# Placing small fp32 products next to each other on TensorE, with a price for each change of kind in the planner's clock

## The chip, the cores and the metric

The program runs on one core of one Trainium2 chip. The metric is device time of one execution in microseconds (us). The kernel before takes 1213.42 us, the median of 3 runs (1213.35 to 1214.24).

The engines are named as in the profile: PE is TensorE (its matrix products and transposes), PEld its weight loads, DVE VectorE, ACT ScalarE, POOL GpSimd, SP SyncE, whose queue issues the transfers.

## The reference

It is a decoder trunk of two layers on 256 positions of width 1024, in float32. A layer is a half-step SwiGLU feed-forward block, a token mixer with three branches side by side, and a second feed-forward block, with a layer norm behind each:

```python
for i in range(DEPTH):                                   # DEPTH = 2
    x = layer_norm(DN_ALPHA * x + 0.5 * swiglu(x, ...))  # gate, up 1024x2816, down 2816x1024
    h = x @ w_in[i]
    z_gmlp, z_qk, z_v, z_s5, z_gate = split(h)
    y_a = gmlp_mixer(z_gmlp, ...)        # gelu, layer norm, causal 128x128 spatial product per group
    y_b = diff_attention(q, k, v, ...)   # 4 heads, softmax(q1 k1) - lam * softmax(q2 k2), causal, rms norm
    y_c = s5_mixer(z_s5, ...)            # complex diagonal scan over time, then a gated linear unit
    mix = sum_k(sigmoid(z_gate[k]) * (y_k @ w_branch[k])) @ w_out
    x = layer_norm(DN_ALPHA * x + mix)
    x = layer_norm(DN_ALPHA * x + 0.5 * swiglu(x, ...))
```

## The kernel before

All weights pass once through the core, 202 blocks ("pairs") of 128x2048 numbers. One transfer brings a block into `raw`; ACT rounds it to fp32r (`wh`, two casts), DVE subtracts to get the remainder (`wl`, two subtractions), and PE multiplies in fp32r: activation-high by weight-high, activation-low by weight-high, activation-high by weight-low. These are the main products, nearly all with 512 or 256 columns. They are one stream in a fixed order.

Beside them PE has small products in plain fp32, whose results other engines wait for. These are 128x128 transposes (`trx` of a normed x, `trh` of a feed-forward activation, `trw` in the preparation of the scan, `tra` of softmax weights, `tro` of attention output, `trm` of the mix) and the products of the branches: `psg<-wsT,vn` (the spatial product of gMLP; the other `psg` are main products of the gates), `pss` (attention scores), `po` (weights by values), `bu` (input of the scan), `py` (output of the scan), `pk`. Tiles are named so in the trace; one fp32 product other than a transpose shows as two MATMUL rows there.

The mixer works like this. DVE turns `bu` by a table (`t`), scans it (`gr`, `gi`) and turns it back (`Hr`, `Hi`), in four blocks; each block's `py` needs `Hr` and `Hi`. An attention step is `pss` on PE, masked maxima on DVE (`sm<-pss`), exponentials on ACT, reciprocals and the weighted difference on DVE (`sm<-sm`), `tra` on PE, a copy on ACT (`at`), `po` on PE. There are four steps of two heads each. The gMLP product goes through DVE twice (`psg<-psg,bsr`, `uv<-uv,psg`) before its PSUM bank is free. `bu`, `py`, `pss`, `po` and the gMLP product share four PSUM banks (`acc`, line 329); `pss` and `bu` take two at once.

Which instruction comes next is decided when the program is built. Every piece of work is a Python generator (a stream) that hands out operations. `Scheduler.run` (line 282) keeps a clock per engine, estimates when each stream's next operation could start (`ready`, line 202; durations from `Engine.cost`, line 119), and issues the one that can start first, by priority where they tie. Engines then run their instructions in that order, whatever the chip's real times are; a semaphore makes an instruction wait, and all behind it on its engine. On PE an operation that isn't of the main stream is taken only if the estimate has its operands ready for 0.5 us already (`SLACK`, line 300). A transpose is put at 0.107 us, an fp32 product of n columns at 0.0017 n, times 0.46 where it has at most 64 output rows (lines 125 and 128). Most operations are recorded at line 222, where the call is made, so that groups are told apart by tile.

Of the kernel before, what the change touches and what calls it, by code (L numbers as in the profile page):

```python
# [8 lines left out]
F32 = mybir.dt.float32  # L9
# [27 lines left out]
P_NORM, P_EVAC, P_ATT, P_SSM, P_MAIN, P_PREP = 10, 20, 30, 40, 50, 55  # L37
# [2 lines left out]
P_TURN = 35  # L40
GO = 1

SLACK = 0.5
P_FOLD = P_SSM

# [5 lines left out]
class Op:  # L51


    def __init__(self, eng, calls, cost, ins, outs):
        self.eng, self.calls, self.cost, self.ins, self.outs = eng, calls, cost, ins, outs


class Alloc:
# [91 lines left out]
class Scheduler:  # L150
# [9 lines left out]
    def __init__(self):  # L160
        self.clock = {e: 0.0 for e in self.READY}
        self.streams = []
        self.track = {}
        self.slots = {}
        self.where = {}
        self.index = {}
        self.writer = {}
        self.table = None
        self.seq = 0

    def spawn(self, gen, prio):
# [5 lines left out]
    def times(self, ap):  # L177
# [21 lines left out]
        q = slice(p0 // 32, (p0 + pairs[0][1] + 31) // 32)  # L199
        return arr, q, ix  # L200

    def ready(self, op):
        t = 0.0
        for a in op.ins:
            arr, q, ix = self.times(a)
            t = max(t, arr[0, q, ix].max())
        for a in op.outs:
            arr, q, ix = self.times(a)
            if self.writer.get(a.tensor.name) == op.eng:
                t = max(t, arr[1, q, ix].max())  # L210
            else:
                t = max(t, arr[:, q, ix].max())
        return t + (0.1 if op.eng == "PE" else 0.0)

    def issue(self, op, start):
        for _, kw in op.calls:
            held = TABLES.get(kw.get("func"))
            if held is not None and self.table not in held:
                self.table = held[0]
                start += 1.3  # L220
        for fn, kw in op.calls:
            fn(**kw)  # L222
        end = start + op.cost
        self.clock[op.eng] = end
        done = end + self.READY[op.eng]
        for a in op.ins:
            arr, q, ix = self.times(a)
            v = arr[1, q, ix]
            arr[1, q, ix] = v.clip(min=end)
        for a in op.outs:  # L230
            arr, q, ix = self.times(a)
            arr[0, q, ix] = done
            self.writer[a.tensor.name] = op.eng
# [48 lines left out]
    def run(self):  # L282
        while self.streams:
            moved = True
            while moved:
                before = [(id(s), id(s[2])) for s in self.streams]
                self.streams = [s for s in list(self.streams) if self.settle(s)] + \
                    [s for s in self.streams[len(before):]]
                moved = before != [(id(s), id(s[2])) for s in self.streams]
            if not self.streams:  # L290
                break
            best = {}
            for s in self.streams:
                if isinstance(s[2], Op):
                    rd = self.ready(s[2])
                    st = max(self.clock[s[2].eng], rd)
                    pr = s[1]()
                    if s[2].eng == "PE" and pr > P_MAIN:
                        pr = P_MAIN - 1
                    late = SLACK if s[2].eng == "PE" and pr != P_MAIN and self.clock["PE"] > 25 else 0.0  # L300
                    best.setdefault(s[2].eng, []).append((max(st, rd + late), pr, s[3], s, st))
            assert best, ([(s[0].__name__, getattr(s[2], "tag", s[2])) for s in self.streams], self.where)
            pick = None
            for eng, c in best.items():
                first = min(x[0] for x in c)
                urgent = [x for x in c if x[0] <= first + (self.PATIENCE[eng] if x[1] < P_MAIN else 1e-9)]
                x = min(urgent, key=lambda y: (y[1], y[0], y[2]))
                if pick is None or x[0] < pick[0]:
                    pick = x
            self.issue(pick[3][2], pick[4])  # L310
            pick[3][2] = None
# [1373 lines left out]
```

## Time and profile before

| | |
|---|---|
| median of 3 runs | 1213.42 us |
| the profiled execution | 1213.71 us |
| its span, first to last instruction | 1212.0 us |
| PE busy | 1195.5 us, 99% |
| DVE busy | 941.9 us, 78% |
| ACT busy | 697.9 us, 58% |
| mean granted PE clock | 0.997 |

The profiled execution is 1.7 us longer than its span. Each row of a timeline is one instruction, or several of one kind in a row (x8), with its start, the length to the end of the last, and, where the engine sat idle before it, that time and what ended it. PE's products overlap, so their pace is the distance between two starts.

### The profile page before, as it was taken

What the parts mean: (1) busy time and instruction counts of PE and PEld (TensorE: products, weight loads), DVE (VectorE), ACT (ScalarE), POOL (GpSimd) and SP (SyncE); (2) the same over time, 40 slices, a digit from 0 to 9 for tenths busy, and PEclk for the clock granted to TensorE, in tenths of its full rate; (3) what the DMA queues carried; (4) which work ended last, traced back from release to release, by engine and by line L of the source; (5) the groups of instructions that cost most, each with busy time, mean ns of one, the idle gap of its engine ahead of it and who ended that gap; (6) DMA issues with size and microseconds to landing.
All of it is one profiled execution on the core that took longest, in us unless ns stands there. A gap on an engine that the chain in (4) does not pass through costs nothing.

```text
span 1212.0 us, 17132 instructions
## 1 busy us (share of the span) xinstructions
PE 1195.5 (99%) x6504; PEld 1010.8 (83%) x6504; DVE 941.9 (78%) x1696; ACT 697.9 (58%) x1152; POOL 12.9 (1%) x54
## 2 busy tenths in 40 slices
PE   8999999999999999999999999999999999999997
PEld 7888888888788888888888888888877888888886
DVE  5997678889997899876886556697899888765656
ACT  5556566655765565565665555476476657555450
POOL 1000000000000010000000000000000000000000
PEclk9999999999999999999999999999999999999998
DMA  8747765565537466667565555557554574655541
GB/s 313 243 174 243 259 217 209 205 231 188 178 138 278 148 235 208 225 210 256 181 219 198 205 181 202 174 200 256 196 183 155 184 251 163 219 203 205 176 172 35
DMA packets 42851, 245.93 MB, mean 203 GB/s; under 512 B 4880, under 2 KB 5648, under 8 KB 17424
## 3 DMA queue, kind: packets, MB, share of 16 engines
q1 hardware_dynamic: 42480, 244.31, 57.5%
q8 instruction: 51, 0.84, 0.3%
q10 hardware_dynamic: 288, 0.52, 0.2%
q14 instruction: 32, 0.26, 0.1%
HBM read 233.28 MB, written 11.53 MB: 202 GB/s over the span
## 4 chain that ended last, share of the span: by engine, by line
PE 86%; DVE 8%; ACT 3%; DMA 2%; issue 1%; DVEq 0%; ACTq 0%
PE ac L222 23%; PE puc L222 17%; PE pgc L222 16%; PE psg L222 8%; PE psp L222 4%; PE pg L222 3%; PE pu L222 3%; DVE wl L222 3%; PE psc L222 2%; PE ps L222 2%; PE pva L222 2%; PE pvg L222 2%; PE psq L222 1%; DMA raw<-in_wst_dram 1%; ACT wh L222 1%; PE py L222 1%
## 5 line engine op out<-in xcount | busy, mean ns | idle before, releaser
L222 DVE TENSOR_TENSOR wl<-raw,wh 128x1024 fp32r<-128x1024 f32 (+2 forms) x416 | 483.1, 1189 | 151.5 <-ACT wh L222 148.3
L222 ACT CAST wh<-raw 128x1024 fp32r<-128x1024 f32 (+2 forms) x416 | 414.2, 1024 | 259.5 <-DMA raw<-in_wst_dram 102.2
L222 PE MATMUL puc<-xx,wh 128*128 128x512 f32 x576 | 144.7, 393 | 0.0
L222 PE MATMUL pgc<-xx,wh 128*128 128x512 f32 x576 | 143.9, 392 | 0.0
L222 PE MATMUL ac<-wh,hTl 128*128 128x512 f32 (+1 forms) x374 | 141.5, 378 | 0.0
L222 PE MATMUL ac<-wh,hTh 128*128 128x512 f32 (+1 forms) x374 | 141.2, 378 | 0.0
L222 PE MATMUL ac<-wl,hTh 128*128 128x512 f32 (+1 forms) x374 | 140.9, 377 | 0.0
L222 PE MATMUL psg<-wh,xx 128*128 128x512 f32 x384 | 122.3, 400 | 0.0
L222 PEld LDWEIGHTS pgc<-xx,wh 128*128 128x128 f32 x576 | 105.1, 188 | 19.9
L222 PEld LDWEIGHTS puc<-xx,wh 128*128 128x128 f32 x576 | 103.4, 189 | 18.4
L222 PEld LDWEIGHTS puc<-xx,wl 128*128 128x128 f32 x576 | 78.4, 190 | 5.5
L222 PEld LDWEIGHTS pgc<-xx,wl 128*128 128x128 f32 x576 | 78.5, 190 | 5.4
L222 PEld LDWEIGHTS ac<-wl,hTh 128*128 128x128 f32 x374 | 70.3, 188 | 13.2
L222 PE MATMUL pgc<-xx,wl 128*128 128x256 f32 x576 | 81.3, 283 | 0.0
L222 PEld LDWEIGHTS psg<-wh,xx 128*128 128x128 f32 x384 | 69.2, 188 | 14.3 <-issue 0.7
L222 PEld LDWEIGHTS ac<-wh,hTl 128*128 128x128 f32 x374 | 70.5, 188 | 12.3
L222 PE MATMUL puc<-xx,wl 128*128 128x256 f32 x576 | 80.5, 283 | 0.0
L222 PEld LDWEIGHTS ac<-wh,hTh 128*128 128x128 f32 x374 | 70.5, 188 | 11.9
L222 PE MATMUL psg<-wl,xx 128*128 128x512 f32 x192 | 75.0, 391 | 0.0
L222 DVE TENSOR_TENSOR silc<-pgc,cp 128x256 f32<-128x256 f32 x72 | 30.2, 420 | 22.3 <-ACT cp L222 22.2
L222 ACT COPY cp<-pgc 128x256 f32<-128x256 f32 x72 | 26.7, 371 | 33.2 <-PE pgc L222 33.2
L222 DVE TENSOR_TENSOR up<-puc,cp 128x256 f32<-128x256 f32 x72 | 30.3, 421 | 18.2 <-ACT cp L222 17.8
(229 smaller groups left out, 1742.5 us busy)
## 6 DMA issues: line engine op xcount, KB each, us to landing
raw<-in_wst_dram SPq DMA_DIRECT2D x198, 1024.0 KB, 4.9
lngb<-in_lngb_dram SPq DMA_DIRECT2D x12, 512.0 KB, 5.9
raw<-in_wst_dram SPq DMA_DIRECT2D x16, 256.0 KB, 5.7
tbd<-tabw SPq DMA_DIRECT2D x8, 512.0 KB, 6.5
tab<-tbd SPq DMA_DIRECT2D x8, 512.0 KB, 4.5
wbd<-WB SPq DMA_DIRECT2D x4, 512.0 KB, 8.6
cd<-C SPq DMA_DIRECT2D x4, 512.0 KB, 9.3
cf<-cd SPq DMA_DIRECT2D x8, 256.0 KB, 5.9
```

The lines of the kernel that those rows point to most:

```text
L222: fn(**kw)
```

## The change

An operation of PE whose first operand is plain fp32 is marked as a side operation. The planner remembers whether PE's last operation was one. Where the kind changes, 0.14 us are added to the estimated start of the operation. After a side operation the 0.5 us of `SLACK` are not asked of the next one: what the estimate has ready then follows at once.

```diff
+TURN = 0.14
@@ class Op
         self.eng, self.calls, self.cost, self.ins, self.outs = eng, calls, cost, ins, outs
+        self.side = eng == "PE" and ins[0].dtype == F32
@@ class Scheduler
+    def turns(self, op):
+
+        return op.eng == "PE" and op.side != self.side
@@ def issue
+        if op.eng == "PE":
+            start += TURN if self.turns(op) else 0.0
+            self.side = op.side
         end = start + op.cost
@@ def run
-                    late = SLACK if s[2].eng == "PE" and pr != P_MAIN and self.clock["PE"] > 25 else 0.0
+                    late = SLACK if s[2].eng == "PE" and pr != P_MAIN and self.clock["PE"] > 25 and not self.side else 0.0
```

No operation is added or taken away, and the main products keep their order. What moves is the place of the side operations between them, and, since the planner's clocks move, the order on DVE, ACT and SP. Runs of side operations on PE ("islands") go from 92 to 77, changes of kind from 183 to 153.

PE in the first layer's mixer, before, from the gMLP product to the first `tra` (psg_2701 to psg_2876 are the gates' main products):

```order
L222 MATMUL psg<-wsT,vn 128x128 x4
...
L222 MATMUL psg<-wsT,vn 128x128 x4
...
L222 MATMUL pss<-k,q 128x128 x4
...
L222 MATMUL pss<-k,q 128x128 x4
...
L222 MATMUL psg_2876<-wl,xx 128x512
L222 MATMUL tra<-ident,sm 128x128
```

The same stretch after the change:

```order
L230 MATMUL pss<-k,q 128x128 x4
...
L230 MATMUL psg<-wsT,vn 128x128 x4
L230 MATMUL pss<-k,q 128x128 x4
...
L230 MATMUL psg_2708<-wl,xx 128x512
L230 MATMUL psg<-wsT,vn 128x128 x4
L230 MATMUL tra<-ident,sm 128x128 x2
L230 MATMUL psg_2708<-wh,xx 128x512 x2
```

Where rows are left out there are only main products. Between the first `pss` and the first `tra` stood 36 main products, and now stand 21. The first `pss` now comes before both gMLP products, the second directly behind one of them, and both `tra` directly behind the other.

DVE in the same stretch, before, from the first block's `Hi` on:

```order
L222 TENSOR_TENSOR Hi<-u,v 128x4x128
L222 TENSOR_TENSOR wl<-raw,wh 128x1024
L222 TENSOR_TENSOR uv<-psu,cp 128x256
...
L222 TENSOR_TENSOR psg<-psg,bsr 128x512
L222 TENSOR_TENSOR uv<-uv,psg 128x512
...
L222 TENSOR_TENSOR t_2685<-t_2685,t_2686 128x512
L222 ISA sm,ast<-pss,mask 128x128
```

After:

```order
L230 TENSOR_TENSOR Hi<-u,v 128x4x128
L230 TENSOR_TENSOR wl<-raw,wh 128x1024 x2
...
L230 TENSOR_TENSOR t_2621<-t_2621,t_2622 128x512
L230 TENSOR_TENSOR wl<-raw,wh 128x1024
L230 TENSOR_TENSOR uv<-psu,cp 128x256
L230 ISA sm,ast<-pss,mask 128x128
...
L230 TENSOR_TENSOR psg<-psg,bsr 128x512
L230 TENSOR_TENSOR wl<-raw,wh 128x1024
L230 TENSOR_TENSOR uv<-uv,psg 128x512
```

`Hi` has moved ahead of two `wl` that stood before it. The two DVE steps that free the first gMLP product's bank come behind the maxima of the first scores, with a `wl` between them.

PE at the end of that layer's mixer, before (`trx` transposes the first half of the normed x; ac are the main products of the output projection):

```order
L222 MATMUL ac_3878<-wl,mix 128x512
L222 MATMUL trx<-ident,xr_3782 128x128 x8
L222 MATMUL ac_3877<-wh,mix 128x512 x2
L222 MATMUL ac_3877<-wl,mix 128x512
L222 MATMUL ac_3878<-wh,mix 128x512 x2
```

After:

```order
L230 MATMUL ac_3877<-wh,mix 128x512 x2
L230 MATMUL ac_3877<-wl,mix 128x512
L230 MATMUL ac_3878<-wh,mix 128x512 x2
L230 MATMUL ac_3878<-wl,mix 128x512
L230 MATMUL trx<-ident,xr_3782 128x128 x8
```

`trx` comes six main products later. On DVE the last `mix<-trm,mix`, which the next ac products need, has moved from behind the norm of the first half to before it.

## Rows read from the trace of the kernel before

**Rows 1.** The page, part 1: engine, busy us (share of the span), instructions.

```profile
PE 1195.5 (99%) x6504; PEld 1010.8 (83%) x6504; DVE 941.9 (78%) x1696; ACT 697.9 (58%) x1152; POOL 12.9 (1%) x54
```

**Rows 2.** Waits of PE: engine, tile <- what ended it: us, times, longest.

```profile
PE py L222 <- DVE Hi L222: 1.3, 2, 1.0
...
PE tra L222 <- DVE oss L222: 0.4, 2, 0.2
```

**Rows 3.** Timeline of PE, 604 to 619: start, us, instruction, count [idle before].

```profile
604.55 0.40 PE L222 MATMUL ac<-wl,hTh 128*128 128x512 f32 x1
604.78 1.03 PE L222 MATMUL trx<-ident,xr 128*128 128x128 f32 x8
605.57 0.47 PE L222 MATMUL ac<-wh,hTl 128*128 128x512 f32 x1
605.89 0.39 PE L222 MATMUL ac<-wh,hTh 128*128 128x512 f32 x1
...
616.59 0.60 PE L222 MATMUL trx<-ident,xr 128*128 128x128 f32 x4
616.94 0.71 PE L222 MATMUL pu<-wh,xx 128*128 128x512 f32 x2
617.49 0.40 PE L222 MATMUL pu<-wl,xx 128*128 128x512 f32 x1
```

**Rows 4.** Timeline of PE, 280 to 294: scores, then a transpose with `bu`.

```profile
281.02 0.39 PE L222 MATMUL psg<-wl,xx 128*128 128x512 f32 x1
281.34 0.71 PE L222 MATMUL pss<-k,q 64*128 64x128 f32 x8
281.99 0.73 PE L222 MATMUL psg<-wh,xx 128*128 128x512 f32 x2
282.55 0.40 PE L222 MATMUL psg<-wl,xx 128*128 128x512 f32 x1
...
291.99 0.27 PE L222 MATMUL tra<-ident,sm 128*128 128x128 f32 x1
292.19 1.16 PE L222 MATMUL bu<-uu,wbf 64*128 64x128 f32 x16
293.28 0.72 PE L222 MATMUL psg<-wh,xx 128*128 128x512 f32 x2
```

**Rows 5.** Timeline of PE, 413 to 415: transposes of the first mixer's norm.

```profile
413.34 1.36 PE L222 MATMUL trx<-ident,xr 128*128 128x128 f32 x8
414.97 0.73 PE L222 MATMUL ac<-wh,mix 128*128 128x512 f32 x2 [0.26 <-DVE mix L222]
```

**Rows 6.** Timeline of DVE at 414.

```profile
414.23 0.68 DVE L222 TENSOR_TENSOR mix<-trm,mix 128x512 fp32r<-128x512 f32 x1
```

**Rows 7.** Timeline of DVE, 251 to 290: steps of the first mixer.

```profile
251.06 2.07 DVE L222 TENSOR_TENSOR t<-bu,tab 128x256 f32<-128x256 f32 x6
...
263.70 2.36 DVE L222 TENSOR_TENSOR wl<-raw,wh 128x1024 fp32r<-128x1024 f32 x2
...
266.31 0.69 DVE L222 TENSOR_TENSOR Hi<-u,v 128x512 f32<-128x512 f32 x1
...
282.09 0.29 DVE L222 CUSTOM_DVE_ANT_0 sm<-pss,mask 128x128 f32<-128x128 f32 x1
...
283.20 0.69 DVE L222 TENSOR_TENSOR t<-t,t 128x512 f32<-128x512 f32 x1
...
289.32 0.16 DVE L222 RECIPROCAL ast<-ast 128x1 f32<-128x1 f32 x1
...
289.94 0.60 DVE L222 SCALAR_TENSOR_TENSOR sm<-sm,ast 128x128 f32<-128x128 f32 x2
```

**Rows 8.** The page, part 6: transfers, KB each, median us to landing.

```profile
tab<-tbd SPq DMA_DIRECT2D x8, 512.0 KB, 4.5
```

**Rows 9.** Timeline of PE, 862 to 866: output of the second layer's first scan block.

```profile
864.32 0.44 PE L222 MATMUL py<-Hi,cf 128*64 128x129 f32 x4 [1.05 <-DVE Hi L222]
...
865.84 0.50 PE L222 MATMUL psu<-xx,wh 128*128 128x512 f32 x1
```

**Rows 10.** Timeline of ACT at 288: exponentials of an attention step.

```profile
288.43 0.40 ACT L222 ACTIVATE sm<-sm,ast 128x128 f32<-128x128 f32 x1
```

More of the change, by code (lines that the diff above doesn't have):

```diff
@@ L168, in __init__ @@
         self.table = None
+        self.side = False
         self.seq = 0
```

## Prediction

> **What bounds the kernel now.** Read the page's busy times first: PE is busy 1195.5 us of a span of 1212.0, DVE 78%, ACT 58% [rows 1]. Nothing runs beside PE that could become the bound as a whole. Its work is fixed: the same products run in both kernels, so the time is the sum of the main products' pace, the price of the islands of small fp32 products, and PE's waits. Read the waits of PE next: in the mixers 1.3 us before py and 0.4 us before tra, two of each [rows 2]. There is little to win there and, since PE has no idle time to absorb a delay, anything that makes PE wait is paid in full.
>
> Third, the timeline around an island tells what a change of kind costs. A main product of 512 columns starts 0.23 us after the one before (604.55 to 604.78). Eight transposes start at 604.78 and the next main product at 605.57, 0.79 us; that one takes 0.32 instead of 0.23 until the next start, 0.09 more: 0.88 for the island [rows 3]. Four transposes take 0.35 (616.59 to 616.94), and the two main products behind them 0.55 instead of 0.46, 0.09 more: 0.44 [rows 3]. Two islands of four are 0.88 as well. Within the rounding of 0.02 a change of kind in and out is free beside transposes; the planner now reckons 0.28 for it (2 x 0.14).
>
> **What merging saves.** 15 islands fewer at 0 to 0.04 us each: 0 to 0.6, I take 0.3. For islands of products that use half of the array's rows the price is higher: pss begins 0.32 after the main product before it, 0.09 late; it takes 0.65 until the next main start, and the two behind it 0.56, 0.10 late [rows 4]. So 0.19 of the 0.84 are entry and exit. But the change puts these beside full-array products (pss behind psg, tra behind bu, tra behind pss), and there the same entry is due: in the merge that exists already, one tra starts at 291.99, bu only 0.20 later (a transpose's own pace in rows 3 is 0.79/8 = 0.10), and the main product 1.09 after bu [rows 4]. [...]
>
> **What the moved trx saves.** In the tails of both mixers trx comes before its operand: 1.63 us from its start to the next main product, where rows 3 have 0.79 for the same eight [rows 5]. Part of this is the next product's own wait for mix, which DVE has made only at 414.23 to 414.91 [rows 5, 6]. Now trx stands six main products (6 x 0.23 = 1.4 us) later and that mix is made before the norm. Both waits go: 2 x 0.84 = 1.7. What is late next is the feed-forward block that needs these transposes; 42 main products, over 9 us, stood between, 36 remain, 8 us, against two casts and eight activations of ACT, below 6 us by the pace of 0.40 [rows 10].
>
> **What the mixer loses.** Here the order is made anew. Count from the end of the first Hi (0.0), for which py waits, in the order after the change.
>
> DVE: two wl at 1.15 (2.36 for two, overlapping by some 0.06), uv 0.33, wl: 3.8. Then t of the second block, which needs its table: that transfer can only be issued when the first table has been read (0.7 before 0.0), and lands 4.5 later [rows 8]: 3.9. Eight t at 0.345 (2.07 for six) and a uv: 7.0; sum of t 0.6, wl 1.15, uv 0.33: 9.1. The maxima 1.1 (282.09 to 283.20): 10.2; another sum 0.6, wl, psg 0.7, wl, uv 0.65: 14.4. The reciprocals 0.6 (289.32 to 289.94), a remainder ya of 0.65 that waits for a cast of ACT of about as much: 15.8; the two sm 0.6: 16.4 [rows 7].
>
> PE: py ends 1.5 after Hi (864.32 to 865.84) [rows 9]; 28 main products, twelve of 512 and sixteen of 256 columns, 4.6: 6.1. First pss 0.84: 7.0. Nine main products 2.05: 9.0; psg<-wsT, eight rows of 0.10, about 0.9: 9.9. The second pss needs the two banks of the first; of the four one is held by py (its copies come later on ACT) and one by psg, so it waits for the maxima: 10.2, a wait of 0.3, ends 11.0. Twelve main products 2.7: 13.7. The second psg<-wsT needs the bank that uv frees at 14.4: 0.7 wait, ends 15.3. Then tra needs the two sm, ready at 16.4: 1.1 wait. That makes 2.1 at this place.
>
> From there both engines run on from 16.4. DVE: scan 1.15, psg and uv 1.3, scan 1.15, ya 0.6, maxima 0.9, then four exponentials of 0.40 on ACT, reciprocals and sm 0.75: 7.5 to the second step's last tra. PE: nine main products 2.05, po 0.45, nine more 2.05, bu 1.3: 5.9, and one tra. Waits 1.4 in all. By the same walk the third step waits little (39 main products lie ahead of it), the fourth, where tra, bu, po and tra follow each other at once, about 1.9: there po needs an exponential, a copy and a transpose that come 0.4 late, and the last tra stands behind two scans of 1.15 on DVE. Together 5.4 per mixer; the first py waits about 0.4 and 1.2 in the two layers, as DVE reaches Hi some 2.7 earlier and PE too.
>
> That is 2 x 5.4 + 1.6 = 12.4 of waiting. From it goes what waits now: 1.7 as idle time [rows 2], nearer 3 as the length of the islands (in rows 5 idle shows 0.26 of 0.84; an estimate). I take +9.2.
>
> Why the planner does not see it: it reckons 0.28 per island that PE does not spend, and for bu 8 x 0.0017 x 128 = 1.74 where rows 4 have 1.09 to 1.3. So PE comes to a tra earlier than planned, and the 0.5 us of margin that covered this is gone just where operations now follow each other.
>
> **Sum.** +9.2 (mixers) - 1.7 (trx) - 0.3 (islands) = +7.2, and I take 0.7 off, as each link of the walk was counted at its full length: +6.5. On the profiled execution, 1213.7, which is 0.3 above the median, this gives 1220.2, against the median 1219.9. I say 1220. Bounds: if only the first place of each mixer waits, 2 x 2.1 + 1.6 - 3 - 2.0 = +0.8; if the walk is 20% short and nothing is taken off, 12.4 x 1.2 - 3 - 2 = +9.9, and a wait of a main product on top of it up to +11.
>
> **Rivals.** (a) The planner's clocks are right where it counts, and the new order waits no more than the old. For it: PE waits only 1.7 us in both mixers now, so the estimates have been good. Against it: that was with 0.5 us of margin. Then only -1.7 - 0.3 remain: 1211.4, faster by 0.17%. 13%. It wins if the DVE steps between Hi and the first sm take under 14.3 (where PE would arrive unhindered) instead of 16.4. (b) A change of kind costs what the planner says. 30 changes less at 0.14 are 4.2, with trx 5.9, and no new waits: 1207.5. For it only the 0.19 at pss; against it rows 3. 5%. (c) Main products wait too: in the new order heads come before the wl of later gates on DVE, and if a wl comes late, PE's whole stream stands. Each such wl is 1.15; one or two per mixer beyond the forecast make 1223 to 1226. Against it: by the new order the blocks for a gate are finished 8 us or more ahead of it. 8%. (d) The change hardly acts: the islands outside the mixers stay where they were but for trx and trw, and if the two mixers' waits offset each other with what they had, 1213 to 1214. 8%.
>
> **Chances.** My forecast 66%, with a range of its own from 1216 to 1223. What can be told from no change is 0.2%, 2.4 us. Slower by more than that: the forecast but for its lowest twentieth, and (c): 72%. Within: (d), most of (a), the lowest part of the forecast: 19%. Faster: (b) and a part of (a): 9%. The range that holds 8 in 10 goes from 1213 to 1224.
>
> **What would show it.** In the mixers of the new profile, PE waits before tra for DVE sm (about 1 us each, first in each mixer right behind the second psg<-wsT), before psg<-wsT for DVE uv (0.7), and before the last tra behind bu and po; PE's idle time grows by 9 there. The eight trx at the tails take 0.8. Pairs of merged trx take as long as two islands. The forecast is wrong if DVE makes the first sm before PE arrives, or if main products show a shorter pace after fewer islands.

## The result and the profile after

The changed kernel takes 1222.39 us (median of 4, 1221.61 to 1223.38) against 1213.83 for the kernel before in the same comparison: a ratio of 1.0062, with a 95% interval of 1.0050 to 1.0075. It is slower, within the forecast range and 2.4 us above the forecast. The profiled execution took 1221.61, its span is 1219.9.

The page's first part, which answers to [rows 1], does not give the cause: PE is 2.7 us busier with the same 6504 instructions, so a part of its waiting must be counted as busy: the eight `trx` read 1.36 in [rows 5] and 1.03 in the tail below, where they wait for nothing.

```profile
PE 1198.2 (98%) x6504; PEld 1013.3 (83%) x6504; DVE 943.6 (77%) x1696; ACT 699.4 (57%) x1152; POOL 12.0 (1%) x54
```

The waits of PE (tile, what ended the wait: us, times, longest) answer to [rows 2]. PE now waits 4.3 us before `tra` for `sm`, where nothing waited for `sm` before.

```profile
PE tra L230 <- DVE sm L230: 4.3, 6, 1.2
...
PE py L230 <- DVE Hi L230: 1.6, 4, 0.5
...
PE tra L230 <- DVE inv L230: 0.9, 2, 0.5
PE po L230 <- ACT at L230: 0.8, 2, 0.4
```

Both kernels run the same 5666 main products in the same sequence. The start of one product in both traces therefore tells how far the changed kernel is behind at that point:

| main product, place | behind, us | change |
|---|---|---|
| 1200, ahead of the first mixer | 0.79 | +0.8 |
| 1700, first mixer's side work done | 6.31 | +5.5 |
| 1850, first norm's `trx` | 5.41 | -0.9 |
| 1990, first `trh` of the next block | 4.22 | -1.2 |
| 4000, ahead of the second mixer | 4.19 | 0 |
| 4500, second mixer's side work done | 8.87 | +4.7 |
| 4700, second norm's `trx` | 7.93 | -0.9 |
| 5665, last | 7.90 | 0 |

The mixers lose 10.2, the rest gives back 2.3. The timeline of PE at the first merged step of the first mixer (start, length, instruction, count, idle before) shows the loss in place: eight `psg` rows from 279.39, 0.11 apart, the last at 280.24, put the next start by their pace at about 280.35, and `tra` starts 0.7 later; behind `bu` the two `tra` wait one after the other.

```profile
279.39 1.13 PE L230 MATMUL psg<-wsT,vn 128*128 128x128 f32 x8 [0.21 <-DVE inv L230]
281.02 0.57 PE L230 MATMUL tra<-ident,sm 128*128 128x128 f32 x2 [0.51 <-DVE sm L230]
...
286.43 1.16 PE L230 MATMUL bu<-uu,wbf 64*128 64x128 f32 x16
288.03 0.30 PE L230 MATMUL tra<-ident,sm 128*128 128x128 f32 x1 [0.44 <-DVE inv L230]
288.80 0.30 PE L230 MATMUL tra<-ident,sm 128*128 128x128 f32 x1 [0.47 <-DVE sm L230]
...
315.25 0.38 PE L230 MATMUL tra<-ident,sm 128*128 128x128 f32 x2
315.56 1.16 PE L230 MATMUL bu<-uu,wbf 64*128 64x128 f32 x16
317.12 0.71 PE L230 MATMUL po<-uv,at 128*128 128x128 f32 x4 [0.40 <-ACT at L230]
319.02 0.41 PE L230 MATMUL tra<-ident,sm 128*128 128x128 f32 x2 [1.18 <-DVE sm L230]
```

The timeline of DVE for the last of these waits: the `sm` at 318.39 stands behind two scans, which take 1.13 and 1.12 from their start to the next one.

```profile
315.66 1.22 DVE L230 TENSOR_TENSOR_SCAN gr<-decay,t 128x512 f32<-128x512 f32 x1
316.79 1.20 DVE L230 TENSOR_TENSOR_SCAN gi<-decay,t 128x512 f32<-128x512 f32 x1
317.91 0.14 DVE L230 RECIPROCAL ast<-ast 128x1 f32<-128x1 f32 x1
...
318.39 0.48 DVE L230 SCALAR_TENSOR_TENSOR sm<-sm,ast 128x256 f32<-128x256 f32 x1
```

And the tail of the first mixer, which answers to [rows 5]: the eight `trx` wait for nothing now, 0.79 to the next product instead of 1.63.

```profile
420.99 1.03 PE L230 MATMUL trx<-ident,xr 128*128 128x128 f32 x8
421.78 0.71 PE L230 MATMUL ac<-wh,mix 128*128 128x512 f32 x2
```

### The profile page after: what moved, and what is told of

It is laid out like the page before. It is cut to its first block, busy times and chain, and to the rows that moved or that the text cites. A ratio compares the mean times of both kernels' runs of the same rounds, so it can differ in the third digit from the quotient of the medians.

```text
span 1219.9 us, 17150 instructions
## 1 busy us (share of the span) xinstructions
PE 1198.2 (98%) x6504; PEld 1013.3 (83%) x6504; DVE 943.6 (77%) x1696; ACT 699.4 (57%) x1152; POOL 12.0 (1%) x54
## 4 chain that ended last, share of the span: by engine, by line
PE 79%; DVE 14%; ACT 4%; issue 1%; DMA 1%; ACTq 0%; DVEq 0%
PE ac L230 23%; PE puc L230 17%; PE pgc L230 16%; PE psg L230 5%; DVE wl L230 4%; PE pg L230 4%; PE pu L230 4%; PE psp L230 3%; DVE t L230 2%; PE psc L230 2%; PE psq L230 1%; DVE sm L230 1%; ACT wh L230 1%; PE psl L230 1%; DMA raw<-in_wst_dram 1%
## 5 line engine op out<-in xcount | busy, mean ns | idle before, releaser
L230 PEld LDWEIGHTS psg<-wl,xx 128*128 128x128 f32 x192 | 36.0, 188 | 7.9
```

## Experiments

Ratios are to the kernel before, run beside each on the same chip, with 95% intervals. "Margin" is `SLACK`, "charge" is `TURN`.

**The charge alone.** Changed kernel, margin kept for every side operation:

```
- late = SLACK if ... self.clock["PE"] > 25 and not self.side else 0.0
+ late = SLACK if ... self.clock["PE"] > 25 else 0.0
```

> The planner charges 0.14 us for each change of kind, as in the changed kernel, but every side operation keeps the 0.5 us of margin. 87 islands of small products (92 before, 77 after). In the first mixer the order is like the changed kernel's up to the second psg from wsT (first pss after 1288 main products instead of 1327); from there each second side operation stands one bundle later. Theory P (the prediction's step on the planner: charge and lost margin act together, PE comes to tra earlier than reckoned and the 0.5 us that covered it is gone): with the margin back, waits at about eight places per mixer shrink by up to 0.5 each, so the mixers give back 3 to 5 of their +10.2, and the kernel takes 1216 to 1219. Rival C (the charge alone re-makes the order, and the waits come with that order): at least as slow as the changed kernel, 1221 to 1225. Rival M (the dropped margin alone does it): 1211 to 1214.

1224.60 us, ratio 1.0088 (1.0076 to 1.0101). The charge alone does the whole damage, and the kept margin saves nothing.

**The margin alone.** Changed kernel with `TURN = 0.0`:

> The charge is set to zero, and only the margin is dropped behind a side operation, as in the changed kernel. 81 islands; the order of both mixers stays that of the kernel before but for three mergers in each (tra with tra and bu, twice; tra with po), and trx in the tails stays where it was, before its operand. Theory P: the three merged places of each mixer lose their 0.5, PE waits up to that at each, +1 to +3: 1214 to 1217. Rival C (the charge alone): equal to the kernel before within 0.1%, 1213 to 1214. Rival M (the dropped margin alone): most of the changed kernel's loss is there, 1218 or more.

1214.71 us, ratio 1.0002 (0.9993 to 1.0011): no difference. Eleven islands are merged away, and neither a gain nor a loss follows. The prediction's words that the margin "is gone just where operations now follow each other" name no cause.

**What a change of kind costs.** The kernel before with 288 transposes more, in 72 islands of four (shortened):

```
+ dummy = [transpose(ident) into quarter k of the chunk's second half for k in range(4)]
+ for i, b in enumerate(work):                       # the four bundles of the first half
+     yield bundle((dummy if i == 0 else []) + [b])
```

> The kernel before, with four more transposes of the identity in each of the 72 gate and up chunks of the feed-forward blocks, all four in one island ahead of the chunk's first product; they go to the half that is not yet begun, and are overwritten. 288 transposes more. Expected by all theories: an island of four takes 0.44, so 72 x 0.44 = 31.7 more than before, 1245, if no wait is added.

The same with one transpose ahead of each bundle:

```
+     yield bundle(dummy[i:i + 1] + [b])
```

> The same 288 transposes, but one each ahead of the four bundles of the chunk: 212 islands more than in the run with one island each, the mixers' order the same in both. If a change of kind in and out costs 0 to 0.04 (my prediction): 0 to 8 us longer than that run, an island of one takes 0.11 to 0.14. If it costs 2 x 0.14, as the changed planner charges: 59 us longer, an island of one takes 0.39.

1247.11 and 1245.51 us, one run each: with 212 islands more, the second is 1.6 us shorter, where the charge would make it 59 longer. The timelines of PE show why. First a chunk with one island, then one with four; read from the first transpose to the first product of the second half (left out in the second: one more transpose with the four products behind it):

```profile
471.83 0.60 PE L222 MATMUL pgc<-ident 128*128 128x128 f32 x4
472.18 2.10 PE L222 MATMUL pgc<-xx,wh 128*128 128x512 f32 x8
474.12 1.11 PE L222 MATMUL pgc<-xx,wl 128*128 128x256 f32 x8
475.07 1.09 PE L222 MATMUL pgc<-xx,wh 128*128 128x512 f32 x4
```

```profile
470.86 0.27 PE L222 MATMUL pgc<-ident 128*128 128x128 f32 x1
470.89 1.18 PE L222 MATMUL pgc<-xx,wh 128*128 128x512 f32 x4
471.90 0.27 PE L222 MATMUL pgc<-ident 128*128 128x128 f32 x1
471.93 1.18 PE L222 MATMUL pgc<-xx,wh 128*128 128x512 f32 x4
...
473.53 0.27 PE L222 MATMUL pgc<-ident 128*128 128x128 f32 x1
473.56 0.72 PE L222 MATMUL pgc<-xx,wl 128*128 128x256 f32 x4
474.12 2.00 PE L222 MATMUL pgc<-xx,wh 128*128 128x512 f32 x8
```

3.24 against 3.26: three changes in and out cost 0.02 together. The other chunks without further side work agree: 3.24 in the mean of 66 with one island, 3.25 of 67 with four.

**PE's prices from the trace.** Changed kernel; products of `bu`, `pss`, `psg`, `po` and `py` at lengths read from the trace, charge 0.01:

```
+ held = {"bu0": 0.16, "bu1": 0.16, "pss": 0.214 if n == 128 else 0.318, "psg": 0.4525, "po": 0.23, "py": 0.163}
+ return held.get(name, max(0.0017 * n, 0.04) * ...)
- TURN = 0.14
+ TURN = 0.01
```

> The changed kernel, margin dropped behind side operations, but the planner's costs on PE are those that the trace shows: bu 0.16 a product instead of 0.218, pss 0.214 and 0.318 instead of 0.218 and 0.435, psg from wsT 0.45 instead of 0.218, po 0.23, py 0.163 instead of 0.10, and a change of kind 0.01 instead of 0.14. 89 islands; in the mixers the order is near that of the kernel before. Theory P (the waits came because the planner's clock of PE ran slow by the charge): with a right clock the waits in the mixers go back to those of before or less, 1211 to 1214. Rival D (DVE is simply too late for any order in which side operations follow each other without a margin): the waits stay, 1218 or more.

1222.70 us, ratio 1.0068 (1.0054 to 1.0082). A miss: the loss stays. The waits of PE in this run are again for `sm`, and for other work of DVE:

```profile
PE tra L232 <- DVE sm L232: 3.6, 6, 1.2
...
PE py L232 <- DVE Hi L232: 1.7, 2, 1.4
PE tro L232 <- DVE o L232: 1.4, 4, 0.4
...
PE pss L232 <- DVE uv L232: 1.0, 2, 0.7
```

But PE's clock is not right in this run either. The table asks 0.4525 for one gMLP product (`psg<-wsT,vn`). In the timeline of PE in the kernel before, eight rows, which are four products, take 0.80 to the next main product, and that one and its successor take 0.09 more: 0.90, or 0.226 for each.

```profile
272.41 0.39 PE L222 MATMUL psg<-wl,xx 128*128 128x512 f32 x1
272.64 1.05 PE L222 MATMUL psg<-wsT,vn 128*128 128x128 f32 x8
273.44 0.71 PE L222 MATMUL psg<-wh,xx 128*128 128x512 f32 x2
273.99 0.39 PE L222 MATMUL psg<-wl,xx 128*128 128x512 f32 x1
```

The old price, 0.218, was nearly right; the table's is twice too long and adds 1.8 in each mixer, which has eight of these products. The other four prices of the table agree with that trace, read in the same way: four `pss` take 0.84 (0.21 each; long ones 1.26, 0.315), two `po` 0.45 (0.225), twelve products of `py` 1.95 (0.163), eight of `bu` 1.27 at 248.44 (0.16), though 1.57 at 315.56. So where this document and the expectations speak of right prices or a right clock of PE, here and in the runs below, this one price is wrong.

Another clock is wrong besides. DVE's start-to-start times in the kernel before agree with the planner's prices nearly everywhere (`u` and `v` of 512 columns: 0.60 reckoned and 0.60 measured; `wl` of 1024: 1.13 and 1.14) but at the scan: 0.183 + 512 x 0.00104 = 0.716 reckoned, 1.13 measured.

**Only the scan's price put right.** Changed kernel, charge 0.14:

```
- return 0.183 + n * 0.00104
+ return 0.07 + n * 0.00207
```

> The changed kernel with one number of its planner put right: a scan on DVE over 512 columns at 1.13 us, as the trace shows it start to start, instead of 0.716. There are 16 scans, eight to a mixer, so DVE is reckoned 3.3 us too short in each mixer. The charge of 0.14 stays and makes PE 4 to 5 us too slow in each mixer against some 2 that its other costs are too short. 83 islands; up to the first tra the mixer's order is that of the kernel before again. Theory B (the waits come where the planner's clocks of PE and DVE drift apart; before, both are reckoned too short and the errors cancel): half or more of the drift goes, 1213 to 1218. Rival D (merged islands make PE wait whatever the clocks): 1220 or more. If the price of the change of kind in itself were the cause: 1221 or more.

1239.41 us, ratio 1.0204 (1.0189 to 1.0219): far from what was expected. Up to main product 1576 the run is only 0.4 behind the kernel before; the 13 us of the first mixer arise in one place, the last block of the scan, part of them at a granted clock of PE of 0.50 (see the last section); in the second mixer nearly all arise there too. The waits of PE:

```profile
PE psl L230 <- DVE y5d L230: 6.6, 2, 3.3
PE py L230 <- DVE Hr L230: 4.4, 2, 2.2
PE py L230 <- DVE Hi L230: 3.8, 3, 1.5
```

The planner itself reckons 8.8 us of waiting there: it takes the next operation that is ready and had put the last block behind everything else. This is a bad plan, and it leaves the question to the next run.

**PE's table, and the scan's price right.** The run with PE's prices from the trace, and the scan at 1.13 as well:

> The changed kernel with the planner's costs on PE as in the run with measured costs (change of kind 0.01) and the scan on DVE at 1.13: both clocks right. Margin still dropped behind side operations. 83 islands. Theory B: no drift is left; the mixers wait as little as before, up to 0.5 at merged places: 1211 to 1216, against 1222.7 with PE's costs alone. Rival D: stays at 1220 or more.

1214.67 us, ratio 1.0005 (0.9996 to 1.0013). The whole loss is gone by one number more than in the run that kept it, although PE is still reckoned too slow by the gMLP products.

**Shorter scans in the changed kernel's own order.** Each scan becomes a product of the same operands, reckoned as before, so that every engine's order stays; the running sum is left out:

```
- yield V.tensor_tensor_scan(out=g, data0=d0, data1=s, initial=0.0, op0=ALU.mult, op1=ALU.add)
+ op = V.tensor_tensor(out=g, in0=d0, in1=s, op=ALU.mult); op.cost = 0.716
+ yield op
```

> The changed kernel in exactly its order on every engine, but each of the 16 scans on DVE (1.13 us start to start) is a plain product of the same operands (0.60), while the planner goes on reckoning 0.716. The running sum along the sequence is left out. DVE gets 8 x 0.53 = 4.2 us shorter in each mixer. Theory B (PE waits in the mixers because DVE, 8 x 0.41 behind its reckoning, arrives after PE, which is ahead of its own): most of these waits go, PE's time in each mixer falls by 3 to 4.5, 1213.5 to 1216.5. Rival O (the waits come from the order of side operations on PE, banks and transfers, and DVE's scans are beside the path): 1220 to 1222.5, no change.

1215.95 us, ratio 1.0023 (1.0013 to 1.0033). The timeline of DVE, then that of PE, at the place of the 1.18 us wait:

```profile
313.84 0.69 DVE L230 TENSOR_TENSOR gr<-decay,t 128x512 f32<-128x512 f32 x1
314.44 0.69 DVE L230 TENSOR_TENSOR gi<-decay,t 128x512 f32<-128x512 f32 x1
315.04 0.16 DVE L230 RECIPROCAL ast<-ast 128x1 f32<-128x1 f32 x1
```

```profile
313.75 1.16 PE L230 MATMUL bu<-uu,wbf 64*128 64x128 f32 x16
315.31 0.71 PE L230 MATMUL po<-uv,at 128*128 128x128 f32 x4 [0.41 <-ACT at L230]
316.18 0.41 PE L230 MATMUL tra<-ident,sm 128*128 128x128 f32 x2 [0.15 <-DVE sm L230]
```

The two scans are 1.05 shorter and the wait 1.03. `po`, which waits for ACT, waits as long as it did. The mixers lose 3.2 and 2.8 us less.

**The charge with the scan's price right.** PE's table and the scan's price, `TURN = 0.14`:

> As the run with both clocks right (1214.67), but with the charge of 0.14 for a change of kind put back: the only wrong number left. 85 islands. Theory B: PE is reckoned 5 to 6 us too slow in each mixer (some 21 islands at 0.28), side work is set too early among the main products and PE waits for it by about that: +4 to +6 in each mixer, with the 2 to 3 that the tails give back 1219 to 1224. Rival (the charge is harmless where DVE's scans are reckoned rightly): 1211 to 1215.

1220.03 us, ratio 1.0050 (1.0037 to 1.0062), the mixers 3.9 and 3.2 us longer than in the kernel before, a little less than expected. Against the same run without the charge they are 3.7 longer each: the charge makes PE wait with the scans priced rightly too.

**The kernel before with PE's table alone** (the same table of lengths, no charge, no merging):

> The kernel before, margin of 0.5 for every side operation, no charge, no merging; only the planner's costs on PE are those of the trace (bu, pss shorter; psg from wsT, po, py longer: PE is reckoned some 2 us longer in each mixer). 100 islands. Theory B (in the kernel before, PE and DVE are both reckoned too short in the mixers, by 2 and by 3.3, and the errors cancel): with PE right and DVE still 3.3 short, PE waits 2 to 3 more in each mixer, 1216 to 1220, slower with better numbers. Rival (right costs can only help, what slowed the run with measured costs down was the margin dropped there): 1211 to 1214.

1219.67 us, ratio 1.0044 (1.0030 to 1.0058): slower, with the margin in place. It does not decide between its two expectations, since its numbers are not the better ones: the table makes PE 2.7 slower in each mixer than the kernel before reckons it, and 0.9 is what was due.

**A larger margin.** The kernel before with `SLACK = 1.0`:

> The kernel before with a margin of 1.0 us instead of 0.5 for every side operation, no charge. 100 islands; in the mixers nearly the order of before, each side operation one to three main products later; in the tails trx stands six main products later than before, as in the changed kernel. Theory P: trx no longer waits (1.77 before, 0.89 when it does not: 0.88 at each of two tails, and what follows it, about 3 in all as in the changed kernel's tails), the mixers wait no more than before: 1209 to 1212. Rival (eight islands more cost the 0.28 each that the planner charges): +2.2, so 1212 to 1214. Rival (a later side operation makes DVE and then main products late): 1215 or more.

1210.87 us, ratio 0.9971 (0.9959 to 0.9982): faster than both kernels. PE's timeline at the tail; both `trx` run without a wait:

```profile
414.30 0.60 PE L222 MATMUL trx<-ident,xr 128*128 128x128 f32 x4
414.66 0.71 PE L222 MATMUL ac<-wh,mix 128*128 128x512 f32 x2
...
416.13 0.60 PE L222 MATMUL trx<-ident,xr 128*128 128x128 f32 x4
416.49 0.71 PE L222 MATMUL ac<-wh,mix 128*128 128x512 f32 x2
```

**PE's table, the scan's price right and a margin of 1.0**, side operations merged without margin:

> Both clocks right, side operations follow a side operation without margin, and the margin for the others is 1.0 instead of 0.5, as in the run that was faster than the kernel before (1210.87). 79 islands. Theory B: the mixers wait little, as with both clocks right, and trx in the tails stands later and no longer waits (-3): 1210 to 1212.5. If merging costs waits of its own even with right clocks: 1214 or more.

1211.00 us, ratio 0.9981 (0.9971 to 0.9991): faster than both too, and not told apart from the run with the margin alone.

## Why it came out so

Each plan holds the planner's own start of every product. Beside it stand the measured starts; here the stretch of 500 main products around each mixer (1200 to 1700, 4000 to 4500), in us. The second column is reckoned, not measured; no plan in the table contains a wait in this stretch (the one with the scan's price alone does, and is left out).

How long PE needs here without waits is an estimate: the plan of the kernel before with PE's table reckons 127.5, less the 1.8 of the gMLP products, 125.7. That 127.5 itself is too long shows in the run with the larger margin, which takes 126.6 and 127.1 with its waits. "Errors" adds by how much a plan reckons PE slower than 125.7, and by how much it reckons DVE's eight scans too short, 8 x 0.41 = 3.3 (nothing where their price is right; with short scans they are reckoned 0.9 too long). "Waited" is the measured stretch less 125.7.

| kernel | reckoned | first mixer | second | errors | waited |
|---|---|---|---|---|---|
| before | 124.8 | 127.5 | 128.1 | -0.9 + 3.3 = 2.4 | 1.8, 2.4 |
| before, margin of 1.0 | 124.8 | 126.6 | 127.1 | -0.9 + 3.3 = 2.4 | 0.9, 1.4 |
| margin alone | 124.8 | 127.2 | 128.3 | -0.9 + 3.3 = 2.4 | 1.5, 2.6 |
| changed | 129.9 | 133.0 | 132.8 | 4.2 + 3.3 = 7.5 | 7.3, 7.1 |
| charge alone | 131.3 | 133.8 | 133.9 | 5.6 + 3.3 = 8.9 | 8.1, 8.2 |
| PE's table, changed | 128.0 | 131.9 | 132.4 | 2.3 + 3.3 = 5.6 | 6.2, 6.7 |
| PE's table, before | 127.5 | 129.0 | 130.4 | 1.8 + 3.3 = 5.1 | 3.3, 4.7 |
| PE's table and scan | 127.9 | 127.7 | 127.7 | 2.2 + 0 = 2.2 | 2.0, 2.0 |
| the same, charge 0.14 | 133.7 | 131.4 | 131.4 | 8.0 + 0 = 8.0 | 5.7, 5.7 |
| changed, short scans | 129.9 | 129.8 | 130.0 | 4.2 - 0.9 = 3.3 | 4.1, 4.3 |

Both errors work the same way. A planner that reckons PE too slow puts too few main products ahead of a side operation, and PE reaches it earlier than planned; one that reckons DVE too short expects DVE's results earlier than they come. From the kernel before to the changed one only the first error moves, by exactly the charge: 18 islands at 0.28 = 5.0, none of which PE spends. The stretch grows by 5.5 and 4.7. The scan's price is the second error, and the kernel before has it too.

The sum is a rough one, since a side operation that is ready in time loses nothing by a wrong clock: it is within 1.1 in most rows, but 1.5 too high in one mixer with the larger margin, 1.8 in one with PE's table in the kernel before, and 2.3 in both with the charge and the right scan. (The table rests on the profiled executions; those of the runs with PE's table before, and with the charge and the right scan, lie some 2 us under their medians.) A run with all of PE's prices right was not made. What they would do beside the scan's old price is therefore open; by the sum PE would wait 3.3, 0.9 more in each mixer than in the kernel before.

Point by point:

- **The turn is free: right.** 0.02 for three of them in the experiment, so the 0.3 put down for the islands was not there either. `psg` with `pss`, 128-row beside 64-row products, gains nothing by the merge, and the prediction's "there the same entry is due" holds: one island of both (at 274.54 in the changed kernel) is 1.75 longer than main products alone, apart they were 0.90 and 0.86. (The 0.10 that the prediction finds behind `pss` is no mark of such a border: its rows 3 have 0.09 behind transposes.) The changed kernel's 0.14 is a price for something that cost 0.02 in three changes in and out beside transposes.
- **Waits of `trx`: right.** -1.7 foretold, -0.9 and -0.9 measured. Not foretold: `trh` behind the first mixer no longer waits for `sil` (0.92 before, -1.2), and 0.8 is lost ahead of the first mixer, 0.7 of it by the tenth main product, which no experiment took apart. That these two nearly offset each other is luck.
- **The walk through the mixer: right in kind, +9.2 against +10.2.** In the first mixer the first place waited 1.3 instead of 2.1 (`pss` did not wait for banks), the second 1.4 as foretold (`po` 0.3, `bu` with `tra` 1.1), the third 0.4 ("little"), the fourth 1.85 against 1.9. `tro` and the last `py` wait 0.55 and 0.6 and were missed. The 0.7 that was taken off at the end had no ground, and 12.4 less 3 is 9.4.
- **The reason: holds in one of its three parts.** "It reckons 0.28 per island that PE does not spend" is the cause: the charge alone brings the loss, and 5.0 reckoned became 5.5 and 4.7. "For `bu` 1.74 where rows have 1.09 to 1.3" is true, but another price errs the other way: `py` 1.21 reckoned and 1.95 measured; in sum the kernel before reckons PE 0.9 too short, not too long. "The 0.5 us of margin is gone" plays no part. The scans were in the walk at their measured 1.15 and nobody asked what the planner took them for: they are the other 3.3 of the errors in each mixer, and as short products in the same order they take 3.2 and 2.8 off.

The two prices, on 512 columns: 1.13 between starts for the scan in the changed kernel, and 0.60 for the product in its place in the run with short scans.

Of the rivals, (a) failed because the planner's clocks were not right where it counted; (b) because the turn costs next to nothing (0.02 for three); (c) and (d) did not show: in the waits of PE no main product of the changed kernel waits for `wl`.

## What to carry to other kernels

When a change adds a price to a scheduler's table, compare every price on both engines that meet there with start-to-start times of the trace before judging the new one. Errors on two engines add up: PE's table cost a ratio of 1.0068 with the scan's old price and 1.0005 with the right one. Count how many products a group of rows holds before it becomes a price: here one was taken twice too long, in five runs. A plan that reckons a stretch without waits longer than a trace shows it with them, as 127.5 against 126.6, gives such a price away. A merge is worth what a change of kind costs, so measure that first: the same instructions in one island and in four. Where a late operand is the trouble, a margin in front of the operation is the cheaper means (0.9971 here).

## What the runs showed of the chip

In the run with the scan's price alone PE waited 2.19, 1.32 and 3.29 us within 12 us; the timeline of PE has the first two so:

```profile
375.38 0.61 PE L230 MATMUL py<-Hr,cf 128*64 128x129 f32 x4 [2.19 <-DVE Hr L230]
377.31 0.70 PE L230 MATMUL py<-Hi,cf 128*64 128x129 f32 x4 [1.32 <-DVE Hi L230]
```

Windows of five us (busy time of PE, PEld, DVE, ACT, POOL, then the granted clock):

```profile
370.00:375.00 5.00, 3.19 (x15) 2.30 (x13) 5.00 (x7) 3.94 (x5) 0.00 (x0) 1.00 0.25 107
375.00:380.00 5.00, 3.30 (x25) 1.78 (x25) 4.49 (x6) 0.54 (x1) 0.00 (x0) 0.55 0.63 210
380.00:385.00 5.00, 1.71 (x9) 1.41 (x7) 1.18 (x2) 3.38 (x10) 0.00 (x0) 0.50 0.89 321
385.00:390.00 5.00, 5.00 (x27) 5.00 (x28) 0.00 (x0) 0.82 (x2) 0.00 (x0) 0.58 0.25 100
390.00:395.00 5.00, 5.00 (x32) 4.47 (x31) 3.16 (x4) 3.54 (x7) 0.00 (x0) 1.00 0.38 91
```

The granted clock reads 1.00 in the first of these windows and 0.50 in the third. If it had only these two values, the mean of 0.55 leaves 4.5 of the second window's 5 us to the lower one (an estimate), so it changed at about 375.5, right behind the first of these waits, which ended at 375.38. In the last window it reads 1.00 again; by then PE had run `psl` products without a wait since 384.94. A `psl` product of 256 columns took 0.21 to the next start at 385.53 and 0.12 at 391.43. In the changed kernel, where PE's waits in the mixers reached 1.18, the clock reads 1.00 in every window of five us from 15 to 1210, the stretch of the longest one among them:

```profile
315.00:320.00 5.00, 3.41 (x30) 2.59 (x29) 4.96 (x12) 2.21 (x7) 0.00 (x0) 1.00 0.64 244
```
